# A two-layer hybrid mixer step: score products of two mixer groups in unbroken runs on row strips of TensorE, and two exponentials queued later

## The chip, the cores and the metric

The kernel runs on one core of one Trainium2 chip, in one launch. The metric is the device time of that launch in microseconds. Before the change it is 1653.74 us, the median of three runs between 1653.5 and 1653.74 us.

## The reference, cut to what matters

One inference step of a two-layer backbone: 256 context tokens and 1024 latent tokens (1280 tokens, ten chunks of 128) of width 1024. Each layer normalises and modulates the tokens, projects them with one wide weight matrix, runs three groups of recurrent heads in two directions, normalises and gates their outputs, and projects back. What the change touches:

```python
# A: mLSTM, 4 heads x 128; the gate rows are cumulated, maximised, exponentiated
m_i = jnp.maximum(a_in, jnp.max(D, axis=3))
wD, wa = jnp.exp(D - m_i[:, :, :, None]), jnp.exp(a_in - m_i)
h = num / jnp.maximum(jnp.abs(den), jnp.exp(-m_i))[..., None]
# B: retention, 4 heads x 64 (key and value width 64)
scores = jnp.einsum('bnihd,bnjhd->bnhij', qc, kc) * jnp.transpose(decay, (2, 0, 1))
# C: gated linear attention, 4 heads, key width 32, value width 64
log_a = jax.nn.log_sigmoid(clr @ gla_w2 + gla_b2) / GLA_TAU      # rank 16 -> the decays
scores = jnp.einsum('bnihd,bnjhd,bnijhd->bnhij', qc, kc, jnp.exp(diff))
```

## The kernel before, in words

The kernel is written as a list of steps per layer (`ORDER`). In layer 0 it begins `g v0 cq ck m d k1 C q0 k0 o0 a0`, in layer 1 `g cq v0 ck m q0 d C k0 k1 o0`. `g` is the projection of the gates and of C's values (L534), `v0` the projection of two heads' values (`mm_tm`, L466), `cq`, `ck`, `k1`, `q0` and others are feature projections (`mm_fm`, L454), `m` the recurrence of group A's gate rows (`mlstm_rows`), `d` the decays of C (`decays`), `C` and `B` the two groups, `a0` one head of A. A planner with a model of the engines' times orders the instructions of each engine's queue; the queues then run in that order. Projections are marked `late()`, which lowers their priority by 20,000 places, so that they fill TensorE wherever a step of a group is not ready. An f32 product stands in the trace as two MATMUL records.

Large tiles come from an arena `f5` of 12 buffers, taken and given back first in, first out; `m` takes five of them, and `d` takes its own from those that `m` gives back. PSUM has two banks for projections (`pj`) and a ring of six (`mx`) for everything else. Weights pass through two buffers `raw`, are split on ScalarE (L415) and VectorE (L416) into a high and a low part, and are then used. `gates_w` loads its weights in three pieces, so the third piece waits for a buffer of the first.

In `m`, VectorE makes the rows `r`, `wa`, `m`; ScalarE takes three exponentials of 36 x 1280 (L581 `wa`, L592 into `TR`, L593 of `-m`); TensorE transposes `TR` in ten blocks of 128 rows (L598) and `m` in ten blocks of 36 rows (L603), and VectorE copies what is needed to `ccol` and `ecol` (L599, L605). `wa` also goes to DRAM (L589).

In C the 128 partitions of `k[p]` and `q[p]` hold, for each direction, two heads of 32. The scores of a chunk are four products over 64 partitions and 256 columns (L827): `qm` holds `q[p]` twice, once with the rows of each head set to zero by POOL (L818) and ScalarE (L819). They go into two banks, one for each direction, are masked on VectorE (L830, L831), and are multiplied with the values (L838). In B the scores of a pair of chunks are eight products over 64 partitions and 128 columns (L1042) into two banks, one for each head of a partition half. The decays are products over the first 64 partitions of `G` (L653).

Nothing holds the products of one such group together in TensorE's queue; the planner puts projections and other products between them.

Of the kernel before, what the change touches and what calls it, by code (L numbers as in the profile page):

```python
# [18 lines left out]
P = 128  # L19
# [69 lines left out]
def hybrid_step(ctx: ExitStack, tc: tile.TileContext, A, O):  # L89
# [46 lines left out]

    def late():

        return tc.high_priority(offset=-LATE)
# [9 lines left out]
    heads_of = cp.tile([P, 2], F32, name="heads_of")  # L149
    for i in range(4):  # L150
        h = slice(32 * i, 32 * i + 32)
        pool.memset(heads_of[h, 0:1], 1.0 - i % 2)
        pool.memset(heads_of[h, 1:2], float(i % 2))
# [303 lines left out]

    def mm_tm(w, cs, ks=range(KT)):

        pv = v3(pj(), 256)  # L460
        with late():
            for u, c in enumerate(cs):
                i = 0
                for e, k in enumerate(ks):
                    for wi, xi in TERMS:
                        pe.matmul(pv[:, u, :], lhsT=hchunk(xi, k, c), rhs=w[e // 4][wi][:, e % 4, :],  # L466
                                  start=(i == 0), stop=(i == 23))
                        i += 1
        return pv
# [37 lines left out]
    def gates_w(l):  # L507

        src = A["w_in"][l].rearrange("(k p) n -> p k n", p=P)
        out = []  # L510
        for k in range(0, KT, 3):
            n = min(3, KT - k)
            raw = raw_ring()
            r = v3(raw[:, 0:912], 304)[:, 0:n, :]
            for d, c0, m in ((0, C_CV, 256), (256, C_AG, 16), (272, C_LR, 32)):
                sync.dma_start(r[:, :, d:d + m], src[:, k:k + n, c0:c0 + m])
            hi, lo = split(raw, 1, n * 304)
            out.append((v3(hi[:, 0:912], 304), v3(lo[:, 0:912], 304)))
        return out
# [27 lines left out]
    def mlstm_rows(l, G):  # L547
# [33 lines left out]
        act.activation(wa, wa, AF.Exp)  # L581
# [10 lines left out]
        act.activation(TR[64:100, :], kw, AF.Exp)  # L592
        act.activation(m, m, AF.Exp, scale=-1.0)  # L593
        for c0 in (0, 4, 8):
            n = min(4, NCH - c0)
            ps = mx()
            for j in range(n):
                pe.transpose(ps[:, j * P:(j + 1) * P], TR[:, (c0 + j) * P:(c0 + j + 1) * P], ident)  # L598
            dve.tensor_copy(ccol[:, c0:c0 + n, :, :],  # L599
                            ps[:, 0:n * P].rearrange("p (c g e) -> p c g e", g=4, e=32)[:, :, :, 0:4])  # L600
# [28 lines left out]
    def decays(l, G, general):  # L629

        w2 = v3(sta(), P)[0:64]
# [13 lines left out]
        for p in range(2):  # L645
# [66 lines left out]
    def group_c(l, q, k, B, vt):  # L712
# [99 lines left out]
        for c0 in range(0, NCH, 2):  # L812

            qm = []
            for p in range(2):
                t = rw()
                x = q[p][:, c0 * P:(c0 + 2) * P]
                pool.tensor_scalar(t[:, 0:256], x, heads_of[:, 0:1], None, ALU.mult)  # L818
                act.activation(t[:, 256:512], x, AF.Copy, scale=heads_of[:, 1:2])  # L819
                qm.append(t.rearrange("p (t u i) -> p t u i", t=2, i=P))  # L820
            for u in range(2):
                c = c0 + u
                s = slice(c * P, (c + 1) * P)
                sc = [mx() for d in range(2)]
                for p in range(2):
                    for d, h in enumerate(half):
                        pe.matmul(sc[d][:, 256 * p:256 * p + 256], lhsT=k[p][h, s], rhs=qm[p][h, :, u, :],  # L827
                                  start=True, stop=True)
                PT = v3(rw(), P)
                dve.tensor_tensor(PT, v3(sc[0], P), m2.unsqueeze(1).to_broadcast([P, 4, P]), ALU.mult)  # L830
                dve.copy_predicated(PT, later.unsqueeze(1).to_broadcast([P, 4, P]), v3(sc[1], P))  # L831
                bank = mx()
                for p in range(2):
                    po = bank[:, p * P:(p + 1) * P]
                    pe.matmul(po, lhsT=q[p][:, s], rhs=state(c)[:, p * P:(p + 1) * P], start=True, stop=False)
                    for t in range(2):
                        e = slice(64 * t, 64 * t + 64)
                        pe.matmul(po[:, e], lhsT=PT[:, 2 * p + t, :], rhs=v3(vt[p], 129)[:, c, e],  # L838
                                  start=False, stop=(t == 1))
# [148 lines left out]
    def group_b(l, q, k, DW, DT, wq, vt):  # L988
# [45 lines left out]
        for c0 in range(0, NCH, 2):  # L1034

            sc = [mx().rearrange("p (u r i) -> p u r i", u=2, i=P) for t in range(2)]
            for u in range(2):
                s = slice((c0 + u) * P, (c0 + u + 1) * P)
                for r in range(2):
                    for t in range(2):  # L1040
                        e = slice(64 * t, 64 * t + 64)
                        pe.matmul(sc[t][:, u, r, :], lhsT=k[r][e, s], rhs=q[r][e, s], start=True, stop=True)  # L1042
# [4 lines left out]
            for u in range(2):  # L1047
# [10 lines left out]
                for r in range(2):  # L1058
# [7 lines left out]
                    for t in range(2):  # L1066
                        pe.matmul(o[:, 64 * t:64 * t + 64], lhsT=PT[t][:, u, r, :], rhs=vv[r][:, c, 64 * t:64 * t + 64],
                                  start=False, stop=(t == 1))
# [381 lines left out]
```

## Time and profile before

| | us |
|---|---|
| median of three runs | 1653.74 |
| the profiled execution, its own time | 1656.08 |
| its span in the trace | 1654.1 |
| TensorE busy (share of the span) | 1588.9 (96%) |
| VectorE busy | 984.9 (60%) |
| ScalarE busy | 615.7 (37%) |
| GpSimd busy | 153.1 (9%) |

PE is TensorE's products, PEld its weight loads, DVE VectorE, ACT ScalarE, POOL GpSimd, SP the queue that issues DMAs. L827 is line 827 of the kernel. A busy TensorE is not one at its peak: the ends of products are modelled, and a record's length holds the way through the array, so intervals between starts tell more than lengths. PEclk is the granted clock as a share of 2.4 GHz.

### The profile page before, as it was taken

To read this page: it belongs to the slowest core of one execution; us is meant where nothing else is said; L and a number is where in the kernel's file an instruction comes from. 1 tells how busy PE (TensorE), PEld (TensorE's weight loads), DVE (VectorE), ACT (ScalarE), POOL (GpSimd) and SP (SyncE) were. 2 spreads that over 40 slices of the span, in tenths; PEclk is the share of its full clock that TensorE was granted. 3 is DMA by queue.
4 is the path that set the end of the run, shared out by engine and by line. 5 is a ranking of instruction groups with operands and counts; after the bars stand their busy time and mean duration, and the time that the engine had idled before them with its cause. 6 is when DMAs were issued, how large, how long until landed. Compare 5 with 4: busy or idle time off the path is not lost.

```text
span 1654.1 us, 28521 instructions
## 1 busy us (share of the span) xinstructions
PE 1588.9 (96%) x10874; PEld 1430.0 (86%) x10874; DVE 984.9 (60%) x2516; ACT 615.7 (37%) x1605; POOL 153.1 (9%) x243
## 2 busy tenths in 40 slices
PE   6889999999999999999999899999999999899997
PEld 2887879888989998889999777999988989888997
DVE  3576664677779855763455677454537633466545
ACT  5535423434112324342365453244411223434323
POOL 1200221101001101000021012100001100000001
PEclk9998999999999999999999999999999999999999
DMA  9211323544324433561141031423233232435203
GB/s 326 71 41 40 76 66 92 153 144 123 102 82 141 149 111 118 192 187 35 37 160 39 17 87 44 110 84 102 73 96 85 58 93 83 125 105 178 80 13 131
DMA packets 169312, 167.43 MB, mean 101 GB/s; under 512 B 19084, under 2 KB 144940, under 8 KB 169164
## 3 DMA queue, kind: packets, MB, share of 16 engines
q1 hardware_dynamic: 168992, 165.45, 33.5%
q8 instruction: 87, 1.43, 0.4%
q14 instruction: 61, 0.50, 0.1%
q10 hardware_dynamic: 172, 0.05, 0.0%
HBM read 129.49 MB, written 27.85 MB: 95 GB/s over the span
## 4 chain that ended last, share of the span: by engine, by line
PE 81%; DMA 7%; DVE 7%; ACT 3%; issue 1%; SPq 0%; POOL 0%; POOLq 0%; DVEq 0%; ACTq 0%
PE pj L454 32%; PE pj L466 26%; PE pj L534 3%; DMA rw<-rrow 2%; PE mx L827 2%; PE mx L1172 2%; PE mx L1121 2%; PE mx L1174 2%; DMA wk<-yd 1%; DVE f L504 1%; DMA f<-f 1%; PE mx L999 1%; PE mx L1042 1%; PE mx L1163 1%; PE mx L292 1%
## 5 line engine op out<-in xcount | busy, mean ns | idle before, releaser
L454 PE MATMUL pj<-hA,hi 128*128 128x256 f32 (+1 forms) x1408 | 369.4, 345 | 0.1
L466 PE MATMUL pj<-hi,hA 128*128 128x256 f32 x1728 | 343.9, 286 | 6.5 <-ACT f L473 2.4
L466 PEld LDWEIGHTS pj<-hi,hA 128*128 128x128 f32 x1728 | 274.7, 189 | 10.8 <-ACT f L473 3.2
L454 PEld LDWEIGHTS pj<-hA,hi 128*128 128x128 f32 x1408 | 242.2, 189 | 30.7 <-issue 2.3
L466 PE MATMUL pj<-hi,hB 128*128 128x256 f32 x1152 | 248.5, 289 | 6.8 <-ACT f L1087 4.4
L454 PE MATMUL pj<-hA,lo 128*128 128x256 f32 (+1 forms) x704 | 238.5, 343 | 0.5 <-DVE lo L416 0.5
L466 PE MATMUL pj<-lo,hA 128*128 128x256 f32 x864 | 236.6, 285 | 0.0
L454 PE MATMUL pj<-hB,hi 128*128 128x512 f32 x704 | 234.8, 403 | 1.7 <-ACT f L473 0.9
L466 PEld LDWEIGHTS pj<-hi,hB 128*128 128x128 f32 x1152 | 193.5, 192 | 9.6 <-ACT f L1087 4.9
L416 DVE TENSOR_TENSOR lo<-raw,hi 128x256 fp32r<-128x256 f32 (+2 forms) x194 | 119.3, 628 | 101.5 <-ACT hi L415 90.0
L466 PE MATMUL pj<-lo,hB 128*128 128x256 f32 x576 | 165.4, 288 | 0.0
L466 PEld LDWEIGHTS pj<-lo,hA 128*128 128x128 f32 x864 | 159.1, 189 | 0.0
L454 PEld LDWEIGHTS pj<-hB,hi 128*128 128x128 f32 x704 | 129.9, 189 | 33.1 <-issue 4.1
L415 ACT CAST hi<-raw 128x256 fp32r<-128x256 f32 (+2 forms) x194 | 107.5, 566 | 135.9 <-PE pj L454 99.1
L454 PEld LDWEIGHTS pj<-hA,lo 128*128 128x128 f32 x704 | 132.7, 189 | 16.2 <-issue 1.0
L454 PE MATMUL pj<-hB,lo 128*128 128x512 f32 x352 | 140.7, 400 | 0.0
L466 PEld LDWEIGHTS pj<-lo,hB 128*128 128x128 f32 x576 | 110.2, 192 | 0.4 <-issue 0.3
L310 DVE SCALAR_TENSOR_TENSOR f<-f,sc 128x256 f32<-128x256 f32 x224 | 96.1, 480 | 16.5 <-DMA f<-in_w_ada_dram 16.2
L473 ACT COPY f<-pj 128x256 f32<-128x256 f32 (+2 forms) x142 | 48.4, 389 | 103.5 <-PE pj L466 48.0
L351 ACT ACTIVATE rw<-f 128x256 bf16<-128x256 f32 (+1 forms) x90 | 43.3, 482 | 107.7 <-DVE f L1343 102.8
L1156 DVE SCALAR_TENSOR_TENSOR rw<-rw,ccol,cst 128x128 f32<-128x128 f32 x160 | 46.7, 347 | 57.1 <-DMA rw<-rrow 56.9
L454 PEld LDWEIGHTS pj<-hB,lo 128*128 128x128 f32 x352 | 66.4, 189 | 15.4 <-issue 1.3
(282 smaller groups left out, 2546.9 us busy)
## 6 DMA issues: line engine op xcount, KB each, us to landing
raw<-in_w_in_dram SPq DMA_DIRECT2D x64, 512.0 KB
f<-in_w_ada_dram SPq DMA_DIRECT2D x32, 384.0 KB
wk<-yd SPq DMA_DIRECT2D x48, 256.0 KB
rw<-rrow SPq DMA_DIRECT2D x40, 256.0 KB
rw<-wrow SPq DMA_DIRECT2D x40, 256.0 KB
f<-in_w_ada_dram SPq DMA_DIRECT2D x16, 512.0 KB
f<-in_x_sample_dram SPq DMA_DIRECT2D x16, 512.0 KB
raw<-in_w_out_dram SPq DMA_DIRECT2D x32, 256.0 KB
```

Of the source, the lines that this page charges most:

```text
L310: dve.scalar_tensor_tensor(acc[v], w, scv[:, k, v:v + 1], acc[v], ALU.mult, ALU.add)
L351: act.activation(rw().bitcast(BF16)[:, 0:x.shape[1]], x, AF.Square, accum_out=out)
L415: act.copy(hi[:, e], raw[:, e])
L416: dve.tensor_tensor(lo[:, e], raw[:, e], hi[:, e].bitcast(F32), ALU.subtract)
L454: pe.matmul(ps[:, :n], lhsT=w[wi][:, k, :], rhs=hblk(xi, k, b), start=(i == 0), stop=(i == 23))
L466: pe.matmul(pv[:, u, :], lhsT=hchunk(xi, k, c), rhs=w[e // 4][wi][:, e % 4, :], start=(i == 0), stop=(i == 23))
L473: act.copy(out, ps)
L534: pe.matmul(ps, lhsT=hchunk(xi, k, c), rhs=w[k // 3][wi][:, k % 3, :], start=(i == 0), stop=(i == 23))
L827: pe.matmul(sc[d][:, 256 * p:256 * p + 256], lhsT=k[p][h, s], rhs=qm[p][h, :, u, :], start=True, stop=True)
L1121: pe.matmul(U[d], lhsT=ks[:, d * P:(d + 1) * P], rhs=v[:, c, :], start=True, stop=True)
L1156: dve.scalar_tensor_tensor(r4[:, d, e, :], r4[:, d, e, :], ccol[:, c0 + e, d, hd:hd + 1], negm[d], ALU.add, ALU.min)
L1172: pe.matmul(po[:, d, :], lhsT=r4[:, d, e, :], rhs=v[:, c, :], start=True, stop=not inter)
```

## The change

1. C's scores: for a pair of chunks, sixteen products over 32 partitions and 128 columns, in the order chunk, `p`, strip `g`, each strip of 32 partitions into a bank of its own (four banks at once). `qm`, `heads_of` and their instructions on POOL and ScalarE go. The four maskings of a pair stay as they are.
2. `run(...)`: the score products of a pair in B (eight) and C (sixteen) get a priority 5,000 places higher, the first waits for the last users of all the banks of the run, and each is ordered behind the one before.
3. The decays are products over all 128 partitions (`w2` is zero where it was not used).
4. In `m`, `exp(-m)` is copied by two DMAs into free rows of `TR`; the ten transposes of 36 rows and their copies go, `ecol` is read from the transposes of `TR`.
5. The three exponentials of `m` are ordered behind the last product of `v0` (layer 0) or the last of its third pair of chunks (layer 1).
6. The third piece of the gates' weights of layer 0 is loaded into a buffer of the arena.

```diff
+    def last_uses(*tiles):
+        names = {t.tensor.name for t in tiles}
+        found = {}
+        for ins in reversed(nc.cur_bb.bb.instructions):
+            if len(found) == 3 * len(names):
+                break
+            if ins.engine in (mybir.EngineType.PE, mybir.EngineType.SP):
+                continue
+            for ap in chain(ins.ins, ins.outs):
+                if hasattr(ap, "bass_ap") and ap.bass_ap.tensor.name in names:
+                    found.setdefault((ins.engine, ap.bass_ap.tensor.name), ins.name)
+        return sorted(set(found.values()))
+
+    @contextmanager
+    def run(*banks):
+        uses, n = last_uses(*banks), len(nc.cur_bb.bb.instructions)
+        with tc.high_priority(offset=LATE // 4):
+            yield
+        mms = nc.cur_bb.bb.instructions[n:]
+        for name in uses:
+            tc.add_manual_dep(mms[0], name, mybir.DependencyInfo(mybir.DependencyClass.Sync, ...
+        for a, b in zip(mms, mms[1:]):
+            tc.add_manual_dep(b, a.name, mybir.DependencyInfo(mybir.DependencyClass.NoSync, ...
...
+    ends = []
+    def not_before(ins, end):
+        tc.add_manual_dep(ins.ins, end.ins.name, mybir.DependencyInfo(mybir.DependencyClass.NoSync, ...
...                      # mm_tm appends its last product to ends
-            raw = raw_ring()
+            raw = f5(1024) if l == 0 and k == 6 else raw_ring()
...
-        act.activation(wa, wa, AF.Exp)
+        not_before(act.activation(wa, wa, AF.Exp), ends[-1 if l == 0 else -3])
...
-        act.activation(TR[64:100, :], kw, AF.Exp)
-        act.activation(m, m, AF.Exp, scale=-1.0)
+        for i in (act.activation(TR[64:100, :], kw, AF.Exp), act.activation(m, m, AF.Exp, scale=-1.0)):
+            not_before(i, ends[-1 if l == 0 else -3])
+        for d in range(2):
+            sync.dma_start(TR[32 * d + 4:32 * d + 8, :], m[32 * d:32 * d + 4, :])
...
-            ps = mx()
-            for j in range(n):
-                pe.transpose(ps[:, j * P:j * P + R], m[:, (c0 + j) * P:(c0 + j + 1) * P], ident[0:R, 0:R])
-            for d in range(2):
-                dve.tensor_copy(ecol[:, c0:c0 + n, d, :], v3(ps[:, 0:n * P], P)[:, :, 32 * d:32 * d + 4])
+            dve.tensor_copy(ecol[:, c0:c0 + n, :, :], pv[:, :, 0:2, 4:8])
...                      # decays
-        w2 = v3(sta(), P)[0:64]
+        w2 = v3(sta(), P)
-                pe.matmul(ps[:, :n], lhsT=w2[:, p, :], rhs=G[0:64, t0:t0 + n], start=True, stop=True)
+                pe.matmul(ps[:, :n], lhsT=w2[:, p, :], rhs=G[:, t0:t0 + n], start=True, stop=True)
...                      # group_c, for each pair of chunks
-            qm = []
-            for p in range(2):
-                t = rw()
-                x = q[p][:, c0 * P:(c0 + 2) * P]
-                pool.tensor_scalar(t[:, 0:256], x, heads_of[:, 0:1], None, ALU.mult)
-                act.activation(t[:, 256:512], x, AF.Copy, scale=heads_of[:, 1:2])
-                qm.append(t.rearrange("p (t u i) -> p t u i", t=2, i=P))
+            sc = [mx() for g in range(4)]
+            with run(*sc):
+                for u in range(2):
+                    s = slice((c0 + u) * P, (c0 + u + 1) * P)
+                    for p in range(2):
+                        for g in range(4):
+                            r = slice(32 * g, 32 * g + 32)
+                            pe.matmul(v3(sc[g], P)[:, 2 * u + p, :], lhsT=k[p][r, s], rhs=q[p][r, s],
+                                      start=True, stop=True, tile_position=(32 * g, 0))
...
-                        pe.matmul(sc[d][:, 256 * p:256 * p + 256], lhsT=k[p][h, s], rhs=qm[p][h, :, u, :],
-                                  start=True, stop=True)
...                      # group_b, for each pair of chunks: the loop as before, inside
+            with run(*sc):
```

## Rows read from the trace of the kernel before

**Rows 1.** The page: busy time by engine, and granted clock in 40 slices.
```profile
PE 1588.9 (96%) x10874; PEld 1430.0 (86%) x10874; DVE 984.9 (60%) x2516; ACT 615.7 (37%) x1605; POOL 153.1 (9%) x243
...
PEclk9998999999999999999999999999999999999999
```

**Rows 2.** The page: chain that ended last, shares of the span.
```profile
PE 81%; DMA 7%; DVE 7%; ACT 3%; issue 1%; SPq 0%; POOL 0%; POOLq 0%; DVEq 0%; ACTq 0%
```

**Rows 3.** Groups by line: xcount | busy us, mean ns | idle before, releaser.
```profile
L827 PE MATMUL mx<-rw,f 64*128 64x256 f32 x160 | 35.7, 406 | 0.0
...
L1042 PE MATMUL mx<-f,f 64*128 64x128 f32 x160 | 18.1, 296 | 0.0
...
L831 DVE COPY_PREDICATED rw<-later,mx 128x512 f32<-128x512 uint8 x20 | 14.5, 726 | 0.4 <-PE mx L827 0.2
L830 DVE TENSOR_TENSOR rw<-mx,masks 128x512 f32<-128x512 f32 x20 | 13.7, 685 | 9.6 <-PE mx L838 9.4
...
L653 PE MATMUL mx<-f,sta 64*128 64x512 f32 (+1 forms) x24 | 12.6, 653 | 0.0
```

**Rows 4.** Timeline of PE in C's loop: start us, us, what, xcount.
```profile
223.96 1.13 PE L827 MATMUL mx<-rw,f 64*128 64x256 f32 x4
225.02 0.50 PE L454 MATMUL pj<-hB,hi 128*128 128x512 f32 x1
225.36 0.39 PE L454 MATMUL pj<-hB,lo 128*128 128x512 f32 x1
```

**Rows 5.** Timeline of PE in B's loop, two visits.
```profile
472.39 1.16 PE L1042 MATMUL mx<-f,f 64*128 64x128 f32 x8
473.47 0.71 PE L999 MATMUL mx<-f,sm 128*128 128x128 f32 x4
...
487.66 1.16 PE L1042 MATMUL mx<-f,f 64*128 64x128 f32 x16
488.75 0.74 PE L454 MATMUL pj<-hA,hi 128*128 128x256 f32 x3
```

**Rows 6.** Timeline of PE at the start: products on four column strips.
```profile
14.57 1.06 PE L292 MATMUL mx<-f,sm 128*32 128x512 f32 x8
```

**Rows 7.** What PE waited for: us in total, times, longest us.
```profile
PE mx L603 <- ACT f L593: 7.2, 2, 3.7
...
PE pj L534 <- ACT hi L415: 4.5, 1, 4.5
```

**Rows 8.** Stretches: us, busy us of PE, PEld, DVE, ACT, POOL, PEclk, DMA share, GB/s.
```profile
50.00:58.00 8.00, 6.16 (x38) 6.13 (x39) 4.37 (x5) 5.05 (x13) 2.38 (x2) 0.79 0.28 70
116.00:140.00 24.00, 20.29 (x73) 14.17 (x72) 5.62 (x20) 10.99 (x15) 0.33 (x3) 0.72 0.04 6
198.00:262.00 64.00, 62.17 (x363) 47.93 (x362) 45.05 (x115) 16.87 (x40) 14.56 (x17) 1.00 0.27 77
469.00:506.00 37.00, 37.00 (x274) 31.25 (x273) 29.94 (x97) 4.49 (x12) 4.61 (x5) 1.00 0.23 65
926.00:940.00 14.00, 10.53 (x57) 8.73 (x56) 5.71 (x20) 8.07 (x10) 0.22 (x2) 0.76 0.06 11
1005.00:1060.00 55.00, 55.00 (x350) 43.85 (x349) 34.06 (x84) 14.49 (x34) 13.06 (x13) 1.00 0.28 75
1266.00:1297.00 31.00, 30.99 (x269) 28.28 (x268) 25.76 (x81) 5.40 (x13) 4.03 (x4) 1.00 0.24 67
```

**Rows 9.** Timeline of ACT in the recurrence of layer 0.
```profile
117.25 1.28 ACT L593 ACT_TABLE_LOAD   x1 [5.15 <-DVE ti L577]
118.54 1.27 ACT L593 ACTIVATE f<-f 36x1280 f32<-36x1280 f32 x1
119.72 1.25 ACT L581 ACTIVATE f<-f 36x1280 f32<-36x1280 f32 x1
121.00 1.27 ACT L592 ACTIVATE f<-f 36x1280 f32<-36x1280 f32 x1
```

**Rows 10.** The chain in order of time: start us, us, what.
```profile
48.30 2.73 DMA raw<-in_w_in_dram
...
161.92 24.02 PE pj L454 x108
...
189.44 2.42 DMA f<-in_state_gla_dram
```

**Rows 11.** What POOL waited for: us in total, times, longest us.
```profile
POOL f L650 <- DMA wrow<-f: 47.3, 1, 47.3
```

More of the change, by code (lines that the diff above doesn't have):

```diff
@@ L1 @@
-from contextlib import ExitStack
+from contextlib import ExitStack, contextmanager
 from itertools import chain
@@ L148, in hybrid_step @@
     negm = [cst[:, K_MF:K_MF + P], cst[:, K_MB:K_MB + P]]
[L149 to L153, printed above, removed]
     masks = cp.tile([P, 256], BF16, name="masks")
@@ L456, in mm_fm @@
         return ps
+    ends = []
+    def not_before(ins, end):
+        tc.add_manual_dep(ins.ins, end.ins.name, mybir.DependencyInfo(mybir.DependencyClass.NoSync,
+                                                                      mybir.DependencyReason.SCHED_ONLY), reason="late")
     def mm_tm(w, cs, ks=range(KT)):
@@ L465, in mm_tm @@
                     for wi, xi in TERMS:
-                        pe.matmul(pv[:, u, :], lhsT=hchunk(xi, k, c), rhs=w[e // 4][wi][:, e % 4, :],
-                                  start=(i == 0), stop=(i == 23))
+                        end = pe.matmul(pv[:, u, :], lhsT=hchunk(xi, k, c), rhs=w[e // 4][wi][:, e % 4, :],
+                                        start=(i == 0), stop=(i == 23))
                         i += 1
+        ends.append(end)
         return pv
@@ L517, in gates_w @@
             hi, lo = split(raw, 1, n * 304)
+            if l == 0 and k == 6:
+                f5.give(raw)
             out.append((v3(hi[:, 0:912], 304), v3(lo[:, 0:912], 304)))
@@ L812, in group_c @@
         for c0 in range(0, NCH, 2):
[L814 to L820 removed]
+            sc = [mx() for g in range(4)]
[7 more added lines that the diff above has]
+                                      start=True, stop=True, tile_position=(32 * g, 0))
+            PT = [v3(rw(), P) for t in range(2)]
+            for t in range(2):
+                dve.tensor_tensor(PT[t], v3(sc[t], P), m2.unsqueeze(1).to_broadcast([P, 4, P]), ALU.mult)
+                dve.copy_predicated(PT[t], later.unsqueeze(1).to_broadcast([P, 4, P]), v3(sc[2 + t], P))
             for u in range(2):
@@ L837, in group_c @@
                         e = slice(64 * t, 64 * t + 64)
[L838 removed]
+                        pe.matmul(po[:, e], lhsT=PT[t][:, 2 * u + p, :], rhs=v3(vt[p], 129)[:, c, e],
                                   start=False, stop=(t == 1))
@@ L1034, in group_b @@
         for c0 in range(0, NCH, 2):
[L1036 to L1042, printed above, removed]
+            sc, v4 = [mx() for t in range(2)], lambda t: t.rearrange("p (u r i) -> p u r i", u=2, i=P)
+            with run(*sc):
+                for u in range(2):
+                    s = slice((c0 + u) * P, (c0 + u + 1) * P)
+                    for r in range(2):
+                        for t in range(2):
+                            e = slice(64 * t, 64 * t + 64)
+                            pe.matmul(v4(sc[t])[:, u, r, :], lhsT=k[r][e, s], rhs=q[r][e, s], start=True, stop=True)
+            sc = [v4(x) for x in sc]
             PT = [rw().rearrange("p (u r i) -> p u r i", u=2, i=P) for t in range(2)]
@@ L1066, in group_b @@
                     for t in range(2):
-                        pe.matmul(o[:, 64 * t:64 * t + 64], lhsT=PT[t][:, u, r, :], rhs=vv[r][:, c, 64 * t:64 * t + 64],
-                                  start=False, stop=(t == 1))
+                        pe.matmul(o[:, 64 * t:64 * t + 64], lhsT=PT[t][:, u, r, :],
+                                  rhs=vv[r][:, c, 64 * t:64 * t + 64], start=False, stop=(t == 1))
                 head_out(bank, 4, c)
```

14 lines of the change are left out of this document (6 added, 8 removed).

## The prediction

> **What bounds the kernel now.** First the page's busy times: TensorE is busy for 96% of the span, VectorE for 60%, and the granted clock is full in nearly every slice [rows 1]. Then the chain that ended last: 81% of it is TensorE [rows 2]. So time taken out of TensorE's queue is time taken off the span, as long as projections are there to move up. Third, where TensorE does less than it could. Its waits are few; two of them concern this change: the ten small transposes L603 wait for an exponential (7.2 us in two stops), and the gates' products wait for the split of a weight piece (4.5 us) [rows 7]. Behind each the granted clock falls to its half level: its mean is 0.72 over 24 us in layer 0, 0.76 over 14 us in layer 1 and 0.79 over 8 us at the start [rows 8], which costs 24 x 0.28 = 6.7, 14 x 0.24 = 3.4 and 8 x 0.21 = 1.7 us.
>
> The rest is hidden inside busy time. Four score records of C take 1.06 us from the first start to the next product's start [rows 4]. In B eight records of 128 columns take 1.08 us, and sixteen take 1.09 [rows 5]. So a 128-column record streams in 0.107 us, two such records on different 64-partition halves run side by side, and on top of 8 x 0.107 = 0.86 us there remain 0.21 us on leaving the strips. The first product behind the visit is 0.50 long against 0.39 for its successor [rows 4], an exposed weight load of 0.11; the first product of the strips pays the same. A visit to row strips thus costs 0.42 us beside its streaming.
>
> I did this sum, end of the product before to begin of streaming of the product after, for every visit in the trace. C: 160 records in 35 visits, 40.3 us, which is 35 x 0.42 = 14.7 for the changes and 25.6 of streaming (34.1 if all were one after another). B: 160 records in 24 visits, 21.0 us: 10.1 and 10.9. Decays: 24 records in 6 visits, 2.5 us of changes.
>
> **The change part by part.** Sums are made against the profiled execution (1656.08 us, span 1654.1); that is 2.3 above the median shown, so a saving is taken from 1653.74.
>
> C's scores. 160 products of 128 columns are 320 records of 0.107, in ten runs of 32. No row shows products on 32-partition strips. From one side: four strips side by side, 8 x 0.107 + 0.42 = 1.28 us a run, 12.8 in all. From the other: all in sequence, 3.42 + 0.42 = 3.84, 38.4 in all. The nearest row: eight records of 512 columns on four column strips take 1.06 us [rows 6], where one alone streams 512 columns in 0.43; they ran four abreast. I take 12.8, a saving of 27.5 us (bounds 2 and 28).
>
> The Trainium skill ("TensorE: Matmul & The Clock Gate", Part 3: Packing small matmuls) gives 3.07 times for four row strips, not 4. By that a run would stream 1.11 instead of 0.86 us and the saving would be 25.0. No run here shows it yet.
>
> The instructions that leave POOL and ScalarE (L818, L819) and the maskings that stay are off TensorE. The maskings matter at the head of a run: it needs four banks, and takes them when the pair before has been masked, 2 x 0.69 + 2 x 0.73 = 2.8 us [rows 3]. What is queued behind a waiting head is all of TensorE. Bounds: 0, as L827 shows 0.0 us of idle before it now [rows 3], and 2.8 for each of the ten runs of C; for B's ten, whose maskings I do not know better, the same. The planner orders the head by its own estimate, which has kept these waits near zero, so I take 0.4 x 20 = 8 us lost, nearer to the row.
>
> B's scores. Ten runs of sixteen records, each as the visit at 487.66 [rows 5]: 0.86 + 0.42 = 1.28, 12.8 in all, saving 8.2 us. If the planner still puts products between, 0 to 8.
>
> Decays. A product over 128 partitions streams the same columns; the six visits fall away: 2.5 us (0 to 3).
>
> The recurrence. The two visits of L603 go, 1.2 us each with the exposed loads: 2.4 us. The stops go only if no other wait takes their place. In layer 0 ScalarE took `-m`, `wa` and `kw` from 118.5 to 122.3 behind a table load [rows 9], all bound by VectorE, while TensorE had already reached L603. Ordered behind the last product of `v0`, the exponentials are planned later: when TensorE stopped, 26 records of `v0` were left (3 us) and some 130 of `cq` and `ck` (over 20 us). The transposes of `TR` now wait for three exponentials and two DMAs on SP's queue; a table load, 3 x 1.27 and a small load like that of 2.42 [rows 10] are 7.5 us behind the last of `v0`. VectorE's chain is shifted by nothing, so in layer 0 they meet data long ready. In layer 1 only 12 records (1.4 us) of the third pair were left at the stop of 3.5 us; planned 1.4 + 7.5 later they are 5 us clear, with 23 us of `v0` and `ck` behind. I take both stops as gone, 7.2 us, and the clock with them, 6.7 + 3.4 = 10.1. Queued behind a late DMA are SP's weight loads, each ahead of its use by a projection. Behind TensorE's transposes nothing waits that is not also behind `v0`. What is late next: the first tile of the decays is the one that held `wa` (POOL's 47.3 us wait for its DMA [rows 11]). If the exponentials came later, decays and C would too; their cover is 24 us of feature projections before C [rows 10]. I put 2 us for what stays of these waits (0 to 17.5, all that was gained here).
>
> The start. With a buffer of its own the third weight piece is issued ahead of loads of tokens; now its last DMA starts at 48.30, 2.73 us before landing [rows 10]. The stop of 4.5 and 1.7 us of clock could go. Behind it stand the second half of the normalised tokens, made on ScalarE and VectorE up to some 54 us, and token loads pushed back by 0.3 MB; I take 4.2 of 6.2 (bounds -1 and 6.2).
>
> Sum: 27.5 + 8.2 + 2.5 + 2.4 + 7.2 + 10.1 + 4.2 = 62.1, less 8 at run heads and 2 in the recurrence: 52. Forecast 1653.74 - 52 = 1602 us. It holds only if TensorE stays fed: in C's loops VectorE has 45 us of work in 64 and 34 in 55, in B's 30 in 37 and 26 in 31 [rows 8]; TensorE would need about 48, 42, 33 and 27, still more than VectorE, though barely.
>
> **The rivals.**
>
> Serial strips: the runs don't overlap, or the planner breaks them. For it: twice as many weight loads for the same scores, and four records of the two halves ran in sequence [rows 4]. Against: the sixteen abreast by two and the eight abreast by four [rows 5, 6]. C's ten runs cost 38.4: 1602 + 25.6 = 1628 us. The Trainium skill (same page, "LDWEIGHTS (loading the stationary operand)") speaks for it: a load's time goes by its 128 columns, not by the partitions. Its Part 3 lets loads overlap where the row group differs, and the pairs in B agree [rows 5]: sixteen records with their loads in 1.09 us.
>
> VectorE becomes the bound of the loops: PSUM is emptied no faster, TensorE's saving turns into idle time. For it: the shares just given. Against: averages below TensorE's. The 35.7 us of C and B, less the 8 already taken off, stay: 1602 + 27.7 = 1630.
>
> The stop moves: transposes of `TR` wait for the third exponential and its DMA. 17.3 us of stops and clock come back: 1619. Against it are the counts of records above.
>
> Slower: every head of the twenty runs stops TensorE for the whole masking, 2.8 us, and every second one is followed by a fall of the clock like that of layer 1 (3.4 us), 4.5 us a head: 1602 - 8 + 90 = 1684. The place is the loops of C and B; it decides from 60 / 20 = 3.0 us a head on, where the gain without heads is used up. For it: four banks of six at once, in a queue that runs in order. Against: 0.0 us of waits there now [rows 3], and k0, k1 and the next products of values to plan between.
>
> **How the numbers follow.** Forecast 0.58 (own range 1588 to 1617), serial strips 0.13, VectorE 0.14, stop moves 0.08, slower 0.07. The best case is all of 62.1 and the start's other 2: 1589. The range 1584 to 1638 holds the forecast and, with some spread, the three cases that end near 1619 to 1630, and leaves out the slow one. About 0.2%, 3 us, is what a measurement of this kernel can tell from no change. All cases but the last are faster; I leave 0.03 for a mix that ends within 0.2%: faster 0.90, same 0.03, slower 0.07.
>
> **What would show it.** C's score line should have 320 records of 32-partition form in ten stretches of about 1.1 us; stretches over 2 us are serial strips. B's line should stand in ten stretches like 487.66. L603 should be gone, no wait above 1 us should stand at L598, and PEclk should be 1.00 from 90 us on in layer 0 and through the recurrence of layer 1. The wait of L534 for its split should be under 1 us. The head of a run should show little idle; if it shows over 1 us on average, or TensorE's busy share in C's loops falls below 90%, the run heads or VectorE have taken the saving. A time above 1638 would make the reading of visits wrong.

## The result and the profile after

The change made the kernel slower: 1665.07 us median (four executions, 1658.01 to 1666.21) against 1653.74; the ratio is 1.006, interval 1.0032 to 1.0088. The forecast was 1602. The profiled execution of the changed kernel is its fastest, 1658.01 us, 1.9 above the profiled one of before; the profile can explain these 1.9 us, and not the other 9 of the medians' difference.

In the listing after the change line numbers are higher: C's scores are L852, its maskings L856 and L857, its products with the state and the values L864 and L867; B's scores L1072; the decays L684; the transposes of a head's output L654; the feature projections L477 and the value projections L496; the exponentials of the recurrence L614 and L625.

The page of the changed kernel, against [rows 1, 2]:

```profile
span 1656.2 us, 28729 instructions
...
PE 1562.5 (94%) x11014; PEld 1423.2 (86%) x11014; DVE 983.5 (59%) x2510; ACT 607.8 (37%) x1587; POOL 128.4 (8%) x215
...
PEclk9999999999999999999999998999999999999999
...
PE 66%; DMA 13%; DVE 12%; ACT 4%; issue 2%; SPq 1%; POOL 0%; DVEq 0%; POOLq 0%; ACTq 0%
```

TensorE's busy time fell by 26.4 us and the span rose by 2.1: TensorE stands idle for 28.5 us more (93.7 against 65.2). The chain that ended last is 66% TensorE, where it was 81%; VectorE and DMAs have taken the difference. Spans and mean granted clock of the two kernels, before first:

```profile
core 0: 1654.1 us, clock 0.987
```

```profile
core 0: 1656.2 us, clock 0.980
```

The part of the clock that was not granted is 1654.1 x 0.013 = 21.5 us before and 1656.2 x 0.020 = 33.1 after. So the busy time at full clock is 1567.4 before and 1529.4 after: 38.0 us of work left TensorE's queue. It came back as 28.5 us of idle time and 11.6 us of half clock behind it.

The saving itself was made where it was forecast. Groups by line of the changed kernel (busy us, mean ns | idle before, releaser), against [rows 3]:

```profile
L852 PE MATMUL mx<-f,f 32*128 32x128 f32 x320 | 12.8, 300 | 2.7 <-DVE rw L857 2.7
...
L1072 PE MATMUL mx<-f,f 64*128 64x128 f32 x160 | 11.6, 285 | 0.2 <-DVE f L1038 0.2
...
L684 PE MATMUL mx<-f,sta 128*128 128x512 f32 (+1 forms) x24 | 10.0, 520 | 0.0
```

A run of C in the timeline of the changed kernel, against [rows 4]:

```profile
189.65 1.17 PE L852 MATMUL mx<-f,f 32*128 32x128 f32 x32
190.80 0.46 PE L864 MATMUL mx<-f,f 128*128 128x128 f32 x2
```

32 records in 1.15 us from first start to the next product's start; six of the other nine runs take 1.10 us, one during which the clock falls to its half level takes 1.71, and behind two the next product itself waits. One after another they would take 3.42 us by the prediction's 0.107 us each: four strips do run abreast. B has ten visits of sixteen records, nearly all as long as the one in [rows 5]:

```profile
468.09 1.16 PE L1072 MATMUL mx<-f,f 64*128 64x128 f32 x16
```

What is new is idle time ahead of other products. The waits of TensorE in the changed kernel (us in total, times, longest), against [rows 7]:

```profile
PE mx L654 <- DVE sm L652: 8.8, 6, 2.2
PE pj L496 <- ACT f L504: 7.6, 7, 4.8
...
PE pj L567 <- ACT hi L438: 4.1, 1, 4.1
...
PE mx L867 <- DVE rw L857: 2.8, 2, 1.5
PE mx L852 <- DVE rw L857: 2.7, 2, 1.9
```

L603 is gone. L654 waits for VectorE's scaling of the heads, L867 and L852 for the maskings. (L504 evacuates the value projections, L567 is the gates' product.) The same loops in stretches of the changed kernel (us, busy us of PE, PEld, DVE, ACT, POOL, PEclk, DMA share, GB/s), against [rows 8]; the third row is C's loop in layer 0, the last one that of layer 1:

```profile
50.00:58.00 8.00, 7.09 (x44) 6.81 (x45) 5.24 (x7) 5.91 (x16) 2.40 (x2) 0.79 0.39 120
116.00:140.00 24.00, 22.70 (x122) 18.77 (x122) 15.52 (x30) 17.89 (x24) 0.33 (x3) 1.00 0.22 52
189.00:252.00 63.00, 54.88 (x502) 49.35 (x501) 43.27 (x111) 13.77 (x35) 10.37 (x12) 0.97 0.32 88
...
1014.00:1055.00 41.00, 34.48 (x315) 30.10 (x314) 27.20 (x63) 6.36 (x14) 5.75 (x6) 0.83 0.22 64
```

TensorE was busy for 97 to 100% of C's loops; now it is for 87 and 84%, at a mean clock of 0.83 in layer 1. These two stretches hold 14.6 of the 93.7 us of idle time, where the loops of before held 1.8. So they account for 12.8 of the 28.5 us that are new; a table below shows where the rest stands. How the loop of layer 1 runs dry shows in TensorE's timeline there:

```profile
1037.05 0.39 PE L477 MATMUL pj<-hB,lo 128*128 128x512 f32 x1
...
1041.77 0.41 PE L654 MATMUL mx<-cst,sm 128*128 128x128 f32 x2 [0.41 <-DVE sm L652]
1044.11 1.61 PE L852 MATMUL mx<-f,f 32*128 32x128 f32 x32 [1.93 <-DVE rw L857]
1047.90 0.66 PE L654 MATMUL mx<-cst,sm 128*128 128x128 f32 x2 [2.19 <-DVE sm L652]
...
1052.81 0.36 PE L496 MATMUL pj<-hi,hA 128*128 128x256 f32 x1
```

From 1037.44, the end of the last L477, to 1052.81 no projection stands in the queue; the longest such stretch in this loop before was 4.8 us (1028.99 to 1033.77). Without projections nothing hides the chain behind a run. VectorE in the same stretch:

```profile
1041.54 1.28 DVE L856 TENSOR_TENSOR rw<-mx,masks 128x512 f32<-128x512 f32 x2
1042.74 1.32 DVE L857 COPY_PREDICATED rw<-later,mx 128x512 f32<-128x512 uint8 x2
1043.95 0.40 DVE L648 TENSOR_REDUCE ti<-sm 128x4 f32<-128x256 f32 x1
1044.39 0.17 DVE L649 TENSOR_SCALAR ti<-ti 128x4 f32<-128x4 f32 x1
1046.28 1.14 DVE L1187 SCALAR_TENSOR_TENSOR rw<-rw,ccol,cst 128x128 f32<-128x128 f32 x4 [1.72 <-DMA rw<-rrow]
1047.34 0.42 DVE L652 TENSOR_TENSOR sm<-mx,ti 128x256 f32<-128x256 f32 x1
```

The mean squares of a head wait behind four maskings, then GpSimd takes its power (1.0 us), and the scaling L652 stands behind an instruction of the next group, which waits for a DMA. TensorE waits for all of it at 1047.90.

### The profile page after: what moved, and what is told of

Read it like the earlier page. It is cut to its first block, busy times and chain, and to the rows that moved or that the text cites. A ratio compares the mean times of both kernels' runs of the same rounds, so it can differ in the third digit from the quotient of the medians.

```text
span 1656.2 us, 28729 instructions
## 1 busy us (share of the span) xinstructions
PE 1562.5 (94%) x11014; PEld 1423.2 (86%) x11014; DVE 983.5 (59%) x2510; ACT 607.8 (37%) x1587; POOL 128.4 (8%) x215
## 4 chain that ended last, share of the span: by engine, by line
PE 66%; DMA 13%; DVE 12%; ACT 4%; issue 2%; SPq 1%; POOL 0%; DVEq 0%; POOLq 0%; ACTq 0%
PE pj L477 25%; PE pj L496 23%; DMA f<-in_w_ada_dram 3%; PE pj L567 3%; DMA rw<-rrow 3%; DMA f<-f 3%; PE mx L1203 2%; PE mx L1152 2%; DVE f L333 2%; DMA wk<-yd 2%; PE mx L1205 2%; PE mx L1194 1%; DVE f L535 1%; DVE lo L439 1%; PE mx L417 1%
## 5 line engine op out<-in xcount | busy, mean ns | idle before, releaser
L477 PE MATMUL pj<-hA,hi 128*128 128x512 f32 (+1 forms) x1408 | 373.3, 347 | 2.3 <-ACT f L504 2.3
L496 PE MATMUL pj<-hi,hA 128*128 128x256 f32 x1728 | 343.6, 286 | 5.7 <-ACT f L1118 2.2
L496 PEld LDWEIGHTS pj<-hi,hA 128*128 128x128 f32 x1728 | 276.3, 190 | 9.5 <-ACT f L1118 2.8
L477 PEld LDWEIGHTS pj<-hA,hi 128*128 128x128 f32 x1408 | 243.4, 191 | 31.1 <-ACT f L504 2.7
L496 PE MATMUL pj<-hi,hB 128*128 128x256 f32 x1152 | 240.4, 287 | 10.3 <-ACT f L504 6.3
L477 PE MATMUL pj<-hB,hi 128*128 128x512 f32 x704 | 237.2, 406 | 4.9 <-ACT f L504 2.5
L496 PE MATMUL pj<-lo,hA 128*128 128x256 f32 x864 | 241.0, 285 | 0.0
L477 PE MATMUL pj<-hA,lo 128*128 128x256 f32 (+1 forms) x704 | 240.7, 346 | 0.0
L496 PEld LDWEIGHTS pj<-hi,hB 128*128 128x128 f32 x1152 | 188.8, 190 | 12.7 <-ACT f L504 7.1
L496 PEld LDWEIGHTS pj<-lo,hA 128*128 128x128 f32 x864 | 161.5, 189 | 0.3 <-issue 0.2
L496 PE MATMUL pj<-lo,hB 128*128 128x256 f32 x576 | 161.6, 285 | 0.0
L477 PEld LDWEIGHTS pj<-hB,hi 128*128 128x128 f32 x704 | 132.4, 192 | 33.7 <-ACT f L504 3.2
L477 PEld LDWEIGHTS pj<-hA,lo 128*128 128x128 f32 x704 | 134.3, 191 | 14.8 <-issue 0.5
L477 PE MATMUL pj<-hB,lo 128*128 128x512 f32 x352 | 142.2, 404 | 0.0
L496 PEld LDWEIGHTS pj<-lo,hB 128*128 128x128 f32 x576 | 108.2, 190 | 0.0
L504 ACT COPY f<-pj 128x256 f32<-128x256 f32 (+2 forms) x142 | 48.5, 390 | 87.7 <-PE pj L496 48.0
L477 PEld LDWEIGHTS pj<-hB,lo 128*128 128x128 f32 x352 | 67.4, 192 | 14.7
L1371 DVE TENSOR_TENSOR wk<-pj,f 128x512 f32<-128x512 f32 (+1 forms) x45 | 28.3, 630 | 83.3 <-PE pj L496 82.6
```

The source lines that it names most:

```text
L477: pe.matmul(ps[:, :n], lhsT=w[wi][:, k, :], rhs=hblk(xi, k, b), start=(i == 0), stop=(i == 23))
L496: end = pe.matmul(pv[:, u, :], lhsT=hchunk(xi, k, c), rhs=w[e // 4][wi][:, e % 4, :], start=(i == 0), stop=(i == 23))
L504: act.copy(out, ps)
L1371: dve.tensor_tensor(t, pv, row.unsqueeze(1).to_broadcast([P, len(cs), 256]), ALU.mult)
```

## The experiments

Two theories to begin with. Theory 1: TensorE's time in the loops of C and B is really saved, but the loops then wait for the chain behind the scores, and no other product is there to put beside it. Theory 2: the form of the run, or TensorE's queue as the planner orders it, costs the time. Ratios are to the kernel before, executed on the same chip in the same batch; its medians there were 1650.15 to 1652.51 us.

**The parts alone.** Each is the kernel before with the lines of one part of the diff above.

```diff
 c_only: + with run(*sc): ... k[p][r, s], q[p][r, s], tile_position=(32 * g, 0)   (C's loop)
 b_only: + with run(*sc): ... k[r][e, s], q[r][e, s]                              (B's loop)
 m_only: + not_before(...), -m by DMA into TR, one transpose                      (recurrence)
 d_only: + w2 = v3(sta(), P); lhsT=w2[:, p, :], rhs=G[:, t0:t0 + n]               (decays)
```

> The kernel before with C's scores alone changed (sixteen products on 32-partition strips in one run for each pair of chunks; no heads_of, no qm). Theory 1, the loop of C is no longer bound by TensorE (projections behind C get their arena tiles only when C gives its own back): TensorE loses about 20 us of work, and less than 5 us of it reach the time, 1649 to 1658. Theory 2, the gain of C is real and another part of the change took it away: 1626 to 1636. Theory 3, the planner's new order costs by itself: above 1658.

> The kernel before with B's score products held together as a run, nothing else. TensorE has 8 us less to do in B's visits. Theory 1 (B's loops become bound by VectorE and by what follows them): 1650 to 1656. Theory 2 (the gain is real, another part took it): 1644 to 1648.

> The kernel before with the recurrence alone changed (three exponentials ordered behind products of v, exp(-m) copied into TR, no transposes of 36 rows). In the changed kernel the stop of layer 0 is gone with its half clock (10.6 us) and in layer 1 a stop of 4.9 and one of 2.5 us stand behind evacuations of v instead. Theory 1 (a stretch behind it eats the gain, as with C): 1650 to 1656. Theory 2 (what is gained in layer 0 is kept): 1640 to 1646. If layer 1's new stop costs more than layer 0 gives: above 1656.

> The kernel before with the decays alone as products over 128 partitions. Six changes of strips less, 2.5 us of TensorE. It is also the nearest to a neutral edit: what the time moves beyond -2.5 us is what a new plan alone does. All theories: 1649 to 1655; a plan that moves the time by itself shows as a shift beyond that.

Measured: c_only 1658.86 us, 1.006 [1.0038, 1.0083]; b_only 1653.56, 1.0028 [1.0013, 1.0042]; m_only 1655.35, 1.0028 [1.0013, 1.0043]; d_only 1650.91, 1.0005 [0.999, 1.002]. No part gains. In c_only the 800th projection record of layer 0 comes 21.8 us earlier than before and the 1000th only 6.4: the gain is made in the loop and lost in its second half and just behind it, with stops of 0.6 to 4.4 us at L646 (the transposes of the head output there). c_only lies at the border of theories 1 and 3, as slow against before as the whole change; m_only has the stop of 4.8 us before the value projections of layer 1 that the changed kernel has (L496 in its list of waits).

**The change without C, and C twice.** In no_c C's loop is that of before; in c_twice each score product is issued twice.

```diff
 no_c:    - with run(*sc): ...  + the qm lines of before (C's loop)
 c_twice: + for twice in range(2):
              pe.matmul(v3(sc[g], P)[:, 2 * u + p, :], ...)
```

> The whole change without the C scores in 32-partition products (their TensorE time is that of before, 35.7 us). Theory 1 (the loop of C has no other product to put beside it, so the 27.5 us that its scores save on TensorE come back as waits for VectorE, ScalarE and the head output, with a half clock behind each): the time is no worse without that part, 1650 to 1660 us. Theory 2 (the parts are additive on TensorE and something else of the change costs some 60 us): without C's saving it is slower still, 1680 us or more.

> The changed kernel with every C score issued twice in a row into the same place: 320 more records, 12.8 us more on TensorE in ten runs of 2.56 us, nothing else changed. Theory 1 (TensorE is not what the loop of C waits for): under 5 us more than the changed kernel, and fewer or shorter stops inside the loop. Theory 2 (TensorE still sets the pace of the loop, the loss is elsewhere): about 12.8 us more than the changed kernel, 1675 to 1680 us.

Measured: no_c 1650.69, 1.0004 [0.9988, 1.002]; c_twice 1673.36, 1.0142 [1.0124, 1.0159]. C's scores are the part that makes the change slower. But c_twice goes theory 2's way and not theory 1's: 0.8% over the changed kernel's ratio is 13.6 us, all that was added. The ten runs took no longer from the first score to the last (31.6 and 28.7 us in its two loops, 32.8 and 30.7 in the changed kernel), and idle time stayed at 92.3 us. The added work pushed projections out of the loops (between the first and the last score stand 30 and 26 projection records, in the changed kernel 76 and 50), and they were paid for later. So the idle time is not slack that any product can use: TensorE's work still adds up, and idle time is put on top of it where the queue, in its order, comes to a product whose input is late.

**Half of C's scores in the kernel before.**

```diff
-pe.matmul(sc[d][:, 256 * p:256 * p + 256], lhsT=k[p][h, s], rhs=qm[p][h, :, u, :],
+pe.matmul(sc[d][:, 256 * p:256 * p + 128], lhsT=k[p][h, s], rhs=qm[p][h, 0, u, :],
```

> The kernel before with 128 of the 256 columns of each C score left out (every second head's scores are read in place of the others, so this part of the result differs); the same number of records in the same order, VectorE's masks as long as before, 17.9 us less on TensorE. Theory 1 (any time saved on TensorE in this loop is given back, whatever its form): 1646 to 1656 us, a ratio over 0.996 to before, with new stops in and after the loop. Theory 2 (it is the run in one piece, waiting for four banks at once, that loses it): most of the 17.9 us is gained, 1634 to 1642 us.

Measured: 1645.98, 0.9974 [0.9959, 0.9989], 4.3 us gained. My 17.9 was too high: the visits take 28.2 us where they took 40.3, so 12.1 were saved, and a good third of that was gained. The time lies at the lower end of theory 1's range. A smaller saving in this loop is partly lost in another form too, but it does not turn into a loss.

**Where the exponentials wait, the run's ties, the transposes' place.** md_l0 is the kernel before with decays and recurrence as changed, held in layer 0 alone; c_norun and a_lt are the whole change with one edit.

```diff
 md_l0:   not_before(...)  ->  if l == 0: not_before(..., ends[-1])
 c_norun: with run(*sc):   ->  if True:                     (C's loop)
 a_lt:    + with late():   around the two pe.transpose of head_out
```

> The kernel before with the decays over 128 partitions, and the recurrence's one-transpose form in both layers, but its exponentials held behind the products of v in layer 0 alone; in layer 1 they are free as before. Theory 1 (layer 0's stop of 7 us and the half clock behind it are cashed where nothing later in the layer waits for another engine, and in layer 1 the holding made a new stop of 5 us): 1642 to 1650 us. Rival (what layer 0 gains is given back before its end, because another chain sets that end): 1650 to 1655 us, a ratio within 0.2% of before.

> The whole change, but the 32 score products of a pair of chunks are not tied into one run: they have the priority of other products again and each waits for its own bank. Theory 1 (TensorE is starved and stopped by what follows the scores, not by the run's form): like the changed kernel, ratio 1.003 to 1.009. Rival (the run taken ahead of everything, waiting for four banks at once, is what costs): ratio under 1.000, 1640 us or less where the changed kernel would be at 1661.

> The whole change, with the two transposes behind each head output of B and C (the line that stopped TensorE for 1.2 to 2.2 us at 206, 224, 246 and 1047 us) given the priority of the projections, so that projections that are ready go ahead of them. Theory 1a (TensorE's in-order queue has the transposes ahead of projections that could run): the stops of 1 to 2.5 us at that line go from layer 0's loop of C, 6 to 12 us with the half clock, ratio 0.999 to 1.003. Theory 1b (there is nothing ready to put there, the chain behind the scores sets the pace): no gain or a loss, ratio 1.005 or more.

Measured: md_l0 1656.42, 1.0035 [1.0017, 1.0054]; c_norun 1665.55, 1.0089 [1.0073, 1.0105]; a_lt 1666.25, 1.0089 [1.0073, 1.0105]. The tie of the run is not the cause, and sending projections ahead of the transposes is no cure. md_l0 gained nothing by freeing the exponentials in layer 1, as the rival had it, but it is 0.35% slower than before, outside the rival's 0.2% too.

**A shorter chain and one more tile.** a_np is the changed kernel without GpSimd's power in the head outputs (1.02 us, 40 times); a13 is the changed kernel with 13 large tiles, made room for by a shorter ring of small ones. b_np and b13 do the same to the kernel before, a_rw5 and b_rw5 shorten the ring alone.

```diff
 a_np, b_np:   - pool.tensor_tensor(ss, ss, mhalf[:, 0:4], ALU.pow)
 a_rw5, b_rw5: - Ring("rw", 8, 512)   + Ring("rw", 5, 512)
 a13, b13:     as a_rw5, b_rw5 and    - f5 = Arena(12)   + f5 = Arena(13)
```

> The whole change with GpSimd's power (1.02 us of each of 40 head outputs of C and B, between two VectorE instructions) left out, so that the heads are scaled by the mean square itself (this part of the result differs). Theory 1 (the chain scores, masks, products, head output, transposes sets the pace of the loops of C now): the stops at the transposes shrink by about 1 us each, 5 to 15 us in all, ratio 0.997 to 1.003. Rival (the pace is set elsewhere, by the arena or by the next step's inputs): ratio 1.004 to 1.008, as the changed kernel.

> The whole change with 13 large tiles instead of 12 (the ring of small working tiles has 5 instead of 8, for the room). Theory 1c (projections that could fill TensorE in the loops of C can't start, since the tiles that they are evacuated into are still held by C): with one more tile one more projection is there beside C, layer 1's stops at 1022 to 1048 us shrink, ratio 0.995 to 1.002. Rival (tiles are not what is missing): within 0.2% of the changed kernel, ratio 1.004 to 1.008.

> The kernel before, with 13 large tiles and a ring of 5 small ones, as the last run had it with the change. Theory 1c (it is the change's shorter loops that lack a tile to evacuate the next projection into): the tile does little for the kernel before, whose TensorE was fed, ratio 0.996 to 1.004, so that with 13 tiles the change is worth 8 to 18 us. Rival (a 13th tile helps any version of this kernel alike): ratio 0.985 to 0.990, and the change costs its 10 us with 13 tiles too.

> The kernel before, with GpSimd's power left out of the head outputs of C and B (this part of the result differs). Theory 1 (the chain behind the scores became the bound only with the change): ratio 0.996 to 1.000, under 6 us gained, against 25 with the change. Rival (the power stood on the path in both): ratio 0.983 to 0.990.

> The whole change with the ring of small tiles cut from 8 to 5 and nothing put in its place (12 large tiles). Theory 1c (the 13th large tile is what let the change be cashed; the shorter ring only costs, about 6 us at the start): ratio 1.006 to 1.014, so that the tile is worth 20 us or more with the change. Rival (it was not the tile: any new plan of the queues moves the time by up to 1% either way, and that run drew a good one): ratio under 1.000, or anywhere between.

> The kernel before with the ring of small tiles cut from 8 to 5 (12 large tiles). Theory 1c (the shorter ring costs, a 13th large tile does nothing for the kernel before): as with 13 tiles, ratio 1.007 to 1.013. Rival (the tile gained something and the ring cost more): ratio over 1.015. If it lies within 0.3% of before, neither explains why 13 tiles made the kernel before 1% slower, and a new plan of the queues did.

| | before | ratio to before | changed | ratio to before |
|---|---|---|---|---|
| as it is | - | 1 | 1665.07 | 1.006 [1.0032, 1.0088] |
| ring of 5 | 1680.40 | 1.0171 [1.0149, 1.0194] | 1668.42 | 1.0103 [1.0087, 1.012] |
| ring of 5, 13 tiles | 1668.89 | 1.0101 [1.0078, 1.0124] | 1641.11 | 0.9942 [0.9921, 0.9963] |
| without the power | 1667.75 | 1.0092 [1.0068, 1.0116] | 1637.54 | 0.9911 [0.9895, 0.9927] |

With the ring as it is the change costs 0.6%. With 13 tiles it gains 1.6 points, 28 us, against b13, without the power 1.8 points, 30 us, against b_np; both of those are 1% slower than the kernel before, which I had not expected of either. The tile is worth 27.3 us to the changed kernel (1668.42 to 1641.11) and 11.5 to the one before, so theory 1c is wrong in that the tile would do nothing there. a_np came out faster than its theory 1 had it, a13 at the fast edge of what theory 1c gave. One part of the tile's worth can be followed, in C's loop of layer 1. TensorE's timeline and one evacuation on ScalarE (L506, of a feature projection) in a_rw5:

```profile
1039.19 0.40 PE L477 MATMUL pj<-hB,lo 128*128 128x512 f32 x1
...
1057.69 0.56 PE L496 MATMUL pj<-hi,hA 128*128 128x256 f32 x1
```

```profile
1053.38 0.60 ACT L506 ACTIVATE f<-pj 128x512 f32<-128x512 f32 x1 [1.22 <-PE mx L864]
```

The same lines in a13, where the scores run from 996.69 to 1028.51:

```profile
1023.82 0.60 PE L496 MATMUL pj<-hi,hA 128*128 128x256 f32 x3
...
1029.29 0.41 PE L654 MATMUL mx<-cst,sm 128*128 128x128 f32 x2 [0.51 <-DVE sm L652]
```

```profile
1019.71 0.60 ACT L506 ACTIVATE f<-pj 128x512 f32<-128x512 f32 x1 [1.68 <-PE pj L477]
```

With 12 tiles the last feature projection ends at 1039.59, and its evacuation starts only at 1053.38, released by a product of C (L864), which reads the tiles that C holds. The value projection L496 follows behind it: 18.1 us without a projection. With 13 tiles the evacuation waits for its own projection alone, and L496 starts inside the loop; the longest stretch without a projection behind it is 3.5 us, and L654 waits 0.5 us, where the changed kernel's longest wait is 2.2. The stretch of a13's loop (columns as above):

```profile
996.00:1040.00 44.00, 40.72 (x387) 36.36 (x385) 27.30 (x64) 7.01 (x17) 6.04 (x6) 0.92 0.19 62
```

93% busy at 0.92, where the changed kernel had 84% at 0.83. The whole run's idle time is 81.2 us (a_rw5 96.2), the clock 0.983 (0.973).

That loop is not all. TensorE's idle time by stretch, in us (a loop of C goes from its first score to 20 us behind the start of its last; each entry is the length of the stretch less TensorE's busy time in it):

| stretch | before | no_c | changed | a_rw5 | a13 | a_np |
|---|---|---|---|---|---|---|
| up to C of layer 0 | 26.8 | 24.1 | 24.7 | 29.2 | 27.1 | 25.3 |
| C of layer 0 | 1.4 | 0.0 | 6.5 | 3.3 | 2.5 | 4.4 |
| from there to B of layer 0 | 2.8 | 5.0 | 12.3 | 10.2 | 5.6 | 3.9 |
| from there to C of layer 1 | 15.3 | 27.0 | 24.0 | 23.3 | 19.8 | 20.7 |
| C of layer 1 | 0.0 | 0.0 | 6.5 | 5.2 | 3.3 | 7.9 |
| behind it | 18.9 | 18.3 | 19.7 | 24.9 | 23.0 | 19.4 |

What the changed kernel has more than no_c, C's part, stands in the two loops (13.0 us) and in the stretch right behind the first one (7.3). What it has more than before on the way to C of layer 1 stands in no_c too, so it belongs to the other parts of the change. The profiled executions of a_rw5 and a13 are 33 us apart. In C of layer 1 idle time and half clock together (0.80 and 0.93 over these 52 us) make about 9 of them; the rest is spread over the other stretches, and which wait the tile took away there was not followed.

The power stands in the same chain. Without it the wait at the transposes is nearly gone, as expected: 8.8 us in the changed kernel, 0.3 in a_np. But C's loop of layer 1 is no better (7.9 us idle, 16.8 us without a projection, a stop of 5.5 us at another product); a_np gains most in the stretch behind C of layer 0. So a loop that runs dry of projections does not by itself make the kernel slower than before. In b_np the same omission made the kernel before 15 us slower, though 41 us of work left GpSimd: new stops of 1.1 to 1.9 us at the same transposes (243 to 257 us), and one of 3.3 at a projection at 364. I had expected up to 6 us gained. An edit that takes work away lets the planner order every queue anew, and in this kernel that alone can cost 1%.

**Versions that beat both.** a13s is a13 with the normalised tokens of layer 0 passed through a free large tile in place of the short ring; a13sl holds the exponentials in layer 0 alone besides.

```diff
 a13s:  - t = rw()[:, :n]   + t = f5(n) if l == 0 else rw()[:, :n]
 a13sl: as a13s, and   not_before(...)  ->  if l == 0: not_before(..., ends[-1])
```

> The whole change with 13 large tiles and a ring of 5 small ones, and in layer 0 the normalised tokens go through a large tile that is free at that time in place of the short ring (the ring of 5 cost about 6 us at 49 to 57 us in the last run). Theory: 4 to 7 us less than that run, 1634 to 1638 us, ratio 0.989 to 0.992. Rival (the start is not on the path, later waits take it back): ratio 0.993 to 0.995.

> As the run with 13 large tiles and the start through them, and the recurrence's exponentials held behind the products of v in layer 0 alone. Theory (holding them in layer 1 delays the evacuation of v by 2 to 5 us at 940 to 970 us): 2 to 5 us less than that run, ratio 0.987 to 0.990. Rival (the freed exponentials stop TensorE elsewhere in layer 1 as they did before): within 0.2% of that run.

Measured: a13s 1645.61, 0.9959 [0.994, 0.9978]; a13sl 1641.18, 0.9932 [0.9908, 0.9955]. The start became worse, not better (the 200th projection 17 us later than before, in a13 6.8): that the large tiles were needed there is likely and was not followed. Against a13s, a13sl gains 4.4 us, as its theory had it. All three with 13 tiles, a13 and a13sl at 1641 us, beat the changed kernel and the kernel before.

## Why the prediction was wrong

**The step that failed** is the sentence under the sum: "It holds only if TensorE stays fed". TensorE did not stay fed: 38.0 us of work left its queue, and 28.5 us of idle time and 11.6 us of half clock took their place. The sum had 10 us for that, 8 at run heads and 2 in the recurrence, and nothing for the products behind a run. I compared VectorE's work in a loop with TensorE's, found TensorE's larger, "though barely", and took the loop as still bound by TensorE. I did not ask what TensorE would do while the chain behind a run is under way. That chain is in sequence: maskings, products, squares, sums, the power, scaling, transposes. It was hidden by projections, and projections need large tiles that C holds. With the scores shorter the loops lacked projections (15.4 us without one in layer 1, where it had been 4.8), and late products stopped the queue. For the loop of layer 1 a13 against a_rw5 shows the tile as the cause: the held evacuation is gone, and some 9 us of idle time and half clock with it. The tile brings 27 us back in all; that the other 18 come about in the same way is not shown. The cause of the 7.3 us behind C of layer 0 is not shown either.

**C's, B's scores and the decays.** 40.6 us with L603's visits, 38.0 of full-clock work measured. Strips: the trace decided for four abreast, 1.10 to 1.15 us at full clock where 8 x 0.107 + 0.21 = 1.07 was expected. The Trainium skill ("TensorE: Matmul & The Clock Gate", Part 3: Packing small matmuls) gives 3.07 times for four row strips, with 512 columns. By that the same stretch would be, as an estimate, 3.42 / 3.07 + 0.21 = 1.32 us; the trace, with 128 columns, does not agree, and the measurement decides.

**Run heads.** 8 us in the sum; 2.7 us measured at L852 and 0.2 at L1072. The planner kept most heads free; the stops came at the products behind the runs.

**The recurrence.** Layer 0 as forecast: no stop at the transposes, PEclk 1.00 in 116 to 140 us. In layer 1 the stop moved, as one rival had it, but to another place than the transposes of `TR`. ScalarE in the changed kernel:

```profile
932.56 3.75 ACT L689 ACTIVATE f<-mx,vT 64x256 f32<-64x256 f32 x6 [6.35 <-DMA rrow<-f]
936.31 1.28 ACT L614 ACT_TABLE_LOAD   x1
937.61 1.27 ACT L614 ACTIVATE f<-f 36x1280 f32<-36x1280 f32 x1
938.90 2.56 ACT L625 ACTIVATE f<-f 36x1280 f32<-36x1280 f32 x2
941.49 1.20 ACT L504 COPY f<-pj 128x256 f32<-128x256 f32 x4
```

The held exponentials stand behind the decays, which wait for a DMA; the evacuation of `v0`, L504, stands behind the exponentials, and TensorE waited 4.8 us for it. I had asked what waits behind TensorE's transposes, not what waits behind the held instructions on ScalarE.

**The clock.** 10.1 us were to come back; 11.6 more were lost, because new stops bring it down again. The 6.7 us of layer 0 were not a property of that stop either. In c_half_before, whose recurrence is that of before, L603 waits the same 3.7 us at 121.55, and 116 to 140 us reads (columns as above; 0.72 in [rows 8]):

```profile
116.00:140.00 24.00, 20.28 (x106) 15.39 (x105) 9.93 (x24) 13.86 (x19) 0.33 (x3) 0.93 0.04 6
```

24 x 0.07 = 1.7 us; b_only and c_only read 0.93 too. This term was sized by one execution.

**The start.** 4.2 us taken, 0.4 found: L567 still waits 4.1 us for its split, PEclk 0.79 as before. Of the piece's three DMAs only the first came earlier (35.13); the two small ones are still issued at 46.20:

```profile
35.13 0.85 SPq L547 DMA_DIRECT2D f<-in_w_in_dram  x1
46.20 1.64 SPq L547 DMA_DIRECT2D f<-in_w_in_dram  x2
```

**The rivals.** "VectorE becomes the bound", where "TensorE's saving turns into idle time", came nearest, but it stopped at a gain of 24 us, and VectorE was not full (27 us of 41 in layer 1). The slower rival had the loop of C as a place, and the falling clock, for the wrong reason: heads of runs cost 2.7 us, not 56. I bounded it by maskings alone and left the chain behind them out.

**What stays open.** How much of the 0.6% is this plan and how much the loop. The loops of C hold under half of the new idle time. Five plans with 12 tiles and the runs or strips of C lie at 1.006 to 1.0103 (the changed kernel, c_only, c_norun, a_lt, a_rw5), so it is hardly one unlucky plan; but b_np shows that a plan alone can cost 1% (d_only, the nearest to a neutral edit, moved by 0.05%), and a13 and a_np, each one plan, may owe a part of their gain to theirs. Why the other executions of the changed kernel are up to 8 us longer than the profiled one is not seen.

## What to carry to other kernels

A busy share near 100% does not say that time taken from that engine is gained: work that fills the engine's waits is part of the share, and here some of it could not start for want of a buffer. Count, beside the busy shares, what may run next to the loop's own chain and which buffers it needs; here one buffer was worth 27 us to the changed kernel. Where a planner orders the queues, try an edit in more than one surrounding before judging it: the same lines were worth +11 us in one and -28 us in another.

## What was not expected of the hardware

Four products on 32-partition strips run abreast: 32 records of 128 f32 columns in 1.10 to 1.15 us, where one after another they would take 3.42. And after the same stop of TensorE, 3.7 us, the clock took 24 x 0.28 = 6.7 us in the execution of the kernel before and 1.7 us in that of c_half_before, a kernel with the same recurrence.
